# Seven block products for the values of two attention groups in a hybrid decoder block on Trainium2

## The chip, the cores and the metric

The kernel runs on one core of a Trainium2 chip. The metric is the device time of one execution in microseconds (us); the time of the kernel before is the median of 3 runs. The engines are named as in the profile: PE multiplies matrices, DVE works on vectors, ACT computes functions and copies, POOL is the general engine, SP issues most of the transfers. PEld is PE's loading of weights, which runs beside its matmuls.

## The reference, cut to what matters

One decoder layer: a SwiGLU half, a token-mixing part, a second SwiGLU half, a final norm. The change is in the token mixing. `u` is 512 tokens by 1024 features, all in float32.

```python
def token_mixing(u, cos, sin, w_in, w_pool, pool_scale, w_pool_branch, w_attn_branch, w_out):
    proj = u @ w_in
    p, q, k, v, gate_logits = jnp.split(proj, cuts, axis=-1)
    y_pool = multiscale_pool(p, w_pool, pool_scale)
    ...
    for gi, (window, dilation) in enumerate(ATTN_PATTERNS):   # (128, 1), (512, 4), (2048, 16)
        hs = slice(gi * HEADS_PER_GROUP, (gi + 1) * HEADS_PER_GROUP)
        o, lse = dilated_window_attention(q[:, :, hs], k[:, :, hs], v[:, :, hs], window // dilation, dilation)
    ...
    gates = jax.nn.sigmoid(gate_logits)
    g_pool, g_attn = jnp.split(gates, N_BRANCHES, axis=-1)
    merged = g_pool * (y_pool @ w_pool_branch) + g_attn * (y_attn @ w_attn_branch)
    return merged @ w_out
```

There are three groups of four heads of 64. The values of groups 2 and 3 are one product: the 512 tokens of `u` by 1024 by 512 columns of `w_in`. The gates are another product of the same `u`, by 2048 columns.

## The kernel before

**Precision.** Every float32 operand is held as a high part and a low part (`UH` and `UL` for `u`, `whi` and `wlo` for weights). A product of two operands is three matmuls: high by high, high by low, low by high.

**Weights.** SP loads them in chunks of 128x1024 into three buffers `raw`. For each chunk ACT writes the high part (line 377) and DVE subtracts it to get the low part (line 389); both go into the ring `whi`/`wlo`. `look(n)` prepares n chunks ahead of the one that PE takes.

**Seven products.** Where the code says `blocks`, a matrix product is split into 2x2 blocks and done by seven block products instead of eight (a Strassen scheme). Four chunks r11, r12, r22, r21 are loaded and seven are used: r11; x0 = r12 + r11; x1 = r22 + x0; r21; r12 + r22; r22; x1 + r21. The first two sums are made on DVE (`make`, line 312). The last two are made by transfers that add to their target and that POOL issues (`add`, line 320): the first when x1 has been made, the second when r21 has been split. The other operand needs four such sums too; `mix_sums` makes them from the parts of `u`: `whole` adds high and low part, `x0`, `x2`, `x1`, `x3` combine the blocks, `hi` and `lo` split the results for PE, and `last` writes the fourth over a block of `UH` and `UL`. A product is 24 matmuls of 128x256; the result of each goes from its bank in PSUM to a copy, since the next product but one accumulates in the same bank.

**Order of the token mixing.** Python code emits it and each engine keeps that order. After the queries and keys of group 1 and its values come eight tiles of 24 matmuls of 128x512 (`mm_tile`): the queries and keys of groups 2 and 3. Two such tiles follow for the pooling; after each, POOL computes `pool_diff` (lines 1573 to 1594). Then come the values of groups 2 and 3: four chunks of 128 tokens, 24 matmuls of 128x512 each (lines 1765 to 1767), with their weights as four chunks held at once; DVE copies each from its bank to `v23` (line 1768). Then come the gates: `gate_duo`, seven products that give two columns of tiles of each gate, four times with branch products between.

**Attention in steps.** The attention of groups 2 and 3 is done in four classes of 128 strided tokens. A class passes through scores on PE (`at_scores`), mask and maximum on DVE and exponentials on ACT (`at_exp`), transposes on PE (`at_turn`, copied by ACT) and values on PE (`at_values`). `hooks` puts the values of one class, the transposes of the next and the scores of a third into one gap between matmuls. Before, class 0 has its scores in the second pooling tile, its transposes in the first chunk of the values and its values in the second; class 3 ends after the first product of the first gate.

**Background.** A row of conditioning products (`bg`, one DVE instruction over 128x1024 and one load each) fills gaps on DVE. A `settle` is a dummy matmul of 128x240 ahead of some products.

Of the kernel before, what the change touches and what calls it, by code (L numbers as in the profile page):

```python
# [18 lines left out]
KT = 8  # L19
# [87 lines left out]
def lay_mix(w_in, w_pb, w_ab, w_out):  # L107
# [16 lines left out]
    for i in range(4):  # L124
        ch.append(v[2 * i:2 * i + 2, :, 256:].transpose(1, 0, 2).reshape(P, -1))
# [40 lines left out]
class Kernel:  # L166
# [6 lines left out]
    def plan(self):  # L173
# [86 lines left out]
        plain(mx[:20])  # L260
# [7 lines left out]
        self.beside = range(base + 4, base + 6)  # L268
# [12 lines left out]
        self.units.update({base + i: T for i in range(16, 20)})  # L281
# [458 lines left out]
    def product(self, bank, u, start, extra=0, other=None):  # L740
# [4 lines left out]
        for p in range(2):  # L745
            o = bank[:, p * HT:(p + 1) * HT]
            for k in range(4):
                (hi, lo), (uh, ul) = w[4 * p + k], u[k]
                M(o, hi, uh, start=start and p == 0 and k == 0, stop=False, skip_group_check=True)  # L749
                M(o, hi, ul, start=False, stop=False, skip_group_check=True)  # L750
                M(o, lo, uh, start=False, stop=k == 3, skip_group_check=True)  # L751
# [557 lines left out]
    def mix_sums(self, xs, x3, slots):  # L1309
# [3 lines left out]
        H, L = {}, {}  # L1313
        four = lambda y: y.rearrange("p (k t) -> p k t", k=4)
        w = xs[:, :2 * D].rearrange("p (k h t) -> p k h t", k=4, h=2)
        x = [four(xs[:, 2 * D:]), w[:, :, 0], w[:, :, 1], four(x3)]

        def copies():
            nc.sync.dma_start(xs[:, :2 * D], self.UHv[:, :2 * D].bitcast(F32))

        def adds():
            nc.gpsimd.dma_start(xs[:, :2 * D], self.ULv[:, :2 * D].bitcast(F32), accum_op=OP.add)

        def whole(i):
            ts = slice(0, HT) if i else slice(HT, T)
            v.tensor_tensor(x[i], *(y.rearrange("p (k t) -> p k t", k=KT)[:, 4:, ts] for y in (self.UHv, self.ULv)), op=OP.add)

        def hi(i):
            H[i] = slots[i][0]()
            nc.scalar.activation(four(H[i]), x[i], AF.Copy)  # L1330

        def lo(i):
            L[i] = slots[i][1]()
            v.tensor_tensor(four(L[i]), x[i], four(H[i]), op=OP.subtract)
            self.S[i] = [H[i], L[i]]
# [4 lines left out]
        def last():  # L1340
            nc.scalar.activation(self.S[3][0], x[3], AF.Copy)
            sub(self.S[3][1], x[3], self.S[3][0])

        self.S = [None] * 3 + [[y.rearrange("p (k t) -> p k t", k=KT)[:, :4, HT:] for y in (self.UHv, self.ULv)]]
        return dict(copies=copies, adds=adds, x0=lambda: sub(x[0], x[0], x[2]), x2=lambda: sub(x[2], x[1], x[2]),
                    x1=lambda: minus(x[1], x[0], x[1]), whole=whole, x3=lambda: minus(x[3], x[3], x[1]), hi=hi, lo=lo, last=last)
# [226 lines left out]
    def pool_diff(self, t, bank):  # L1573
# [4 lines left out]
        if t:  # L1578
            p = self.v23.rearrange("p c f -> p (c f)")[:, 2 * T:2 * T + 528]
# [20 lines left out]
    def pool_map(self, high, low):  # L1600
# [3 lines left out]
        banks = (self.bO, self.bS[0])  # L1604
# [10 lines left out]
    def mix(self):  # L1615
# [8 lines left out]
        xs = mp.tile([P, 3 * D], F32, name="xs")  # L1624
        x = [xs[:, i * D:(i + 1) * D] for i in range(3)]
        two = lambda n: [t[:, i * T:(i + 1) * T] for t in [mp.tile([P, D], F32R, name=n)] for i in range(2)]
# [3 lines left out]
        with tc.tile_pool(name="rt", bufs=1) as self.rt, tc.tile_pool(name="aw", bufs=2) as self.aw:  # L1630
# [22 lines left out]
            self.ada_free, self.ada_stop, self.ada_depth = list(x), 59, 2  # L1653
# [57 lines left out]
            for g in (1, 2):  # L1711
                for dst in (self.qt[g], self.kt[g]):
                    for hp in range(2):
                        more = [(2, self.bg)] if dst is self.qt[1] and hp else []
                        b = self.mm_tile(hooks(todo.pop(0), rest + more + [(7, self.bg)]))
                        rt = [self.scratch(2 * i + hp)[:, :T] for i in range(2)]
                        self.rope_a(b, dst, hp, *rt)

                        rest = [(6, lambda dst=dst, hp=hp, w=rt[1]: self.rope_b(dst, hp, w))]


            g23 = [[(1, c, hp) for hp in range(2)] for c in range(4)]
            b = self.mm_tile(hooks([], rest + [(3, self.bg)]))
            self.pool_diff(0, b)
            assert self.ada_next == 59 and not self.adat, self.ada_next
            self.ada_free, self.ada_stop, self.ada_depth = [self.cs], 60, 1
            self.bg_fetch()
            v4 = []

            def half(i):  # L1730
                if not v4:
                    v4.append(ma.tile([P, 2 * D], F32R, name="v23"))
                return v4[0][:, i * D:(i + 1) * D]

            u = self.mix_sums(xs, self.qt[2], [[wide(ma, "k2"), wide(mp, "uc")], [wide(ma, "k0"), wide(ma, "v1")],
                                                 [lambda: half(0), lambda: half(1)]])
# [4 lines left out]
            assert self.ada_next == 60 and not self.adat, self.ada_next  # L1741
            self.held = self.pos
            w = [x for _ in range(4) for x in self.take()]
# [6 lines left out]
            def free():  # L1750
                self.held += 1
# [445 lines left out]
```

## Time and profile before

| what | before |
|---|---|
| median of 3 runs | 970.66 us (970.06 to 971.09) |
| the profiled execution | 969.99 us |
| its span, first to last instruction | 968.2 us |
| PE busy | 958.5 us (99%) |
| DVE busy | 840.3 us (87%) |
| ACT busy | 539.3 us (56%) |
| POOL busy | 89.8 us (9%) |

The profile comes from one execution. A row of the timeline has the start, the duration, the engine, the line, the operation, output<-inputs with their shape, the number of merged instructions and, in brackets, the idle time before it with what ended it. A row of a group has the busy time in all and the mean of one in ns. Matmuls overlap in PE's pipeline, so what one costs is read from the distance between starts. In the trace, `v` is both `v1` and `v23`, and the last digits of names are left out.

### The profile page before, as it was taken

Reading aid. Unit: us, or ns where it says so; the run is one execution under the profiler, and the core shown is the slowest. Engines: PE = TensorE matmul, PEld = TensorE weight load, DVE = VectorE, ACT = ScalarE, POOL = GpSimd, SP = SyncE. Lnnn points to the kernel's source line nnn. Section 1 sums busy time; section 2 is a strip of 40 time slices with the busy share of each in tenths; the row PEclk is TensorE's granted clock in tenths of the full one; section 3 lists DMA queues with packets and bytes.
Section 4 is the critical chain, followed back from the end, with each engine's and each line's share of the span. In section 5 each row is a group of like instructions: output and inputs, shape, how many; then the busy total and the mean of one; then the engine's idle time right before and its main releaser. Section 6 shows DMA issues by size and latency. Waiting matters only on the chain.

```text
span 968.2 us, 18169 instructions
## 1 busy us (share of the span) xinstructions
PE 958.5 (99%) x7296; PEld 899.9 (93%) x7296; DVE 840.3 (87%) x1237; ACT 539.3 (56%) x813; POOL 89.8 (9%) x106
## 2 busy tenths in 40 slices
PE   9999999999999999999999999999999999999997
PEld 7888999999999899778889998998999999999997
DVE  7989999899998778787897877989799888989886
ACT  5443666665755553444565453365666747566655
POOL 0000110101010003005510000000101000110002
PEclk9999999999999999999999999999999999999999
DMA  9857785776768648766457445723757666665632
GB/s 353 283 178 257 197 239 156 202 212 153 219 176 246 171 148 238 239 206 188 90 141 199 124 126 207 243 73 104 194 141 198 170 157 167 172 171 143 169 83 88
DMA packets 54087, 174.71 MB, mean 180 GB/s; under 512 B 7793, under 2 KB 10481, under 8 KB 53746
## 3 DMA queue, kind: packets, MB, share of 16 engines
q1 hardware_dynamic: 44416, 141.29, 44.2%
q0 software_dynamic: 9008, 31.72, 18.1%
q8 instruction: 57, 0.93, 0.4%
q10 hardware_dynamic: 578, 0.53, 0.2%
q14 instruction: 28, 0.23, 0.1%
HBM read 135.36 MB, written 2.24 MB: 142 GB/s over the span
## 4 chain that ended last, share of the span: by engine, by line
PE 84%; DVE 7%; DMA 4%; issue 2%; ACT 1%; POOL 0%; SPq 0%; POOLq 0%; DVEq 0%; ACTq 0%
PE bank L750 13%; PE bank L749 12%; PE bank L751 12%; PE bank L421 7%; PE bank L422 7%; PE bank L423 7%; PE bank L1109 4%; PE bank L1108 4%; PE bank L1110 4%; DVE wlo L389 2%; PE bank L2119 2%; PE bank L2121 1%; PE bank L2123 1%; DMA v<-wada 1%; DMA cs<-wada 1%
## 5 line engine op out<-in xcount | busy, mean ns | idle before, releaser
L389 DVE TENSOR_TENSOR wlo<-raw,whi 128x1024 fp32r<-128x1024 f32 (+3 forms) x150 | 166.4, 1118 | 37.7 <-ACT whi L377 37.5
L749 PE MATMUL bank<-UH,whi 128*128 128x256 f32 x672 | 185.7, 276 | 0.0
L750 PE MATMUL bank<-UL,whi 128*128 128x256 f32 x672 | 185.6, 276 | 0.0
L751 PE MATMUL bank<-UH,wlo 128*128 128x256 f32 x672 | 185.6, 276 | 0.0
L389 DVE TENSOR_TENSOR wlo<-X,whi 128x1024 fp32r<-128x1024 f32 (+3 forms) x133 | 142.2, 1082 | 17.8 <-ACT whi L377 17.6
L377 ACT ACTIVATE whi<-raw 128x1024 fp32r<-128x1024 f32 (+3 forms) x150 | 142.6, 964 | 22.1 <-DMA raw<-wf1o 8.4
L377 ACT ACTIVATE whi<-X 128x1024 fp32r<-128x1024 f32 (+3 forms) x133 | 123.0, 946 | 51.0 <-DVE X L312 46.1
L750 PEld LDWEIGHTS bank<-UL,whi 128*128 128x128 f32 x672 | 126.3, 188 | 0.0
L749 PEld LDWEIGHTS bank<-UH,whi 128*128 128x128 f32 x672 | 126.1, 188 | 0.2
L751 PEld LDWEIGHTS bank<-UH,wlo 128*128 128x128 f32 x672 | 126.2, 188 | 0.0
L751 PE MATMUL bank<-SH,wlo 128*128 128x256 f32 x408 | 112.7, 276 | 0.2 <-DVE wlo L389 0.2
L749 PE MATMUL bank<-SH,whi 128*128 128x256 f32 x408 | 112.6, 276 | 0.0
L750 PE MATMUL bank<-SL,whi 128*128 128x256 f32 x408 | 112.6, 276 | 0.0
L421 PE MATMUL bank<-UH,whi 128*128 128x512 f32 (+1 forms) x272 | 93.0, 342 | 0.0
L422 PE MATMUL bank<-UL,whi 128*128 128x512 f32 (+1 forms) x272 | 92.0, 338 | 0.0
L423 PE MATMUL bank<-UH,wlo 128*128 128x512 f32 (+1 forms) x272 | 91.8, 337 | 0.0
L751 PEld LDWEIGHTS bank<-SH,wlo 128*128 128x128 f32 x408 | 76.6, 188 | 0.4 <-DVE wlo L389 0.4
L749 PEld LDWEIGHTS bank<-SH,whi 128*128 128x128 f32 x408 | 76.6, 188 | 0.0
L750 PEld LDWEIGHTS bank<-SL,whi 128*128 128x128 f32 x408 | 76.6, 188 | 0.0
L1108 PE MATMUL bank<-HI,whi 128*128 128x256 f32 x224 | 61.8, 276 | 0.0
L1109 PE MATMUL bank<-HK,whi 128*128 128x256 f32 x224 | 61.8, 276 | 0.0
L1110 PE MATMUL bank<-HI,wlo 128*128 128x256 f32 x224 | 61.8, 276 | 0.0
(406 smaller groups left out, 2410.9 us busy)
## 6 DMA issues: line engine op xcount, KB each, us to landing
raw<-wmix SPq DMA_DIRECT2D x44, 512.0 KB, 4.3
raw<-wf1i SPq DMA_DIRECT2D x32, 512.0 KB, 5.9
raw<-wf2i SPq DMA_DIRECT2D x30, 512.0 KB, 4.3
ada<-wada SPq DMA_DIRECT2D x23, 512.0 KB, 5.2
X<-raw POOLq DMA_DIRECT2D x23, 512.0 KB, 6.0
xs<-wada SPq DMA_DIRECT2D x17, 512.0 KB, 5.3
X<-wf2i SPq DMA_DIRECT2D x14, 512.0 KB, 4.5
X<-wf1i SPq DMA_DIRECT2D x11, 512.0 KB, 4.6
```

Of the source, the lines that this page charges most:

```text
L377: self.nc.scalar.activation(self.hi[:, y], r[:, x], AF.Copy)
L389: self.nc.vector.tensor_tensor(self.lo[:, y], r[:, x], self.hi[:, y], op=OP.subtract)
L421: M(ps, hi, uh, start=start, stop=False)
L422: M(ps, hi, ul, start=False, stop=False)
L423: M(ps, lo, uh, start=False, stop=stop)
L749: M(o, hi, uh, start=start and p == 0 and k == 0, stop=False, skip_group_check=True)
L750: M(o, hi, ul, start=False, stop=False, skip_group_check=True)
L751: M(o, lo, uh, start=False, stop=k == 3, skip_group_check=True)
L1108: M(o, hi, uh, start=start and m % 2 == 0 and k == 0, stop=False, skip_group_check=True)
L1109: M(o, hi, ul, start=False, stop=False, skip_group_check=True)
L1110: M(o, lo, uh, start=False, stop=k == 1, skip_group_check=True)
L2119: M(b, hi, self.UH[k], start=k == 0, stop=False)
```

## The change

The values of groups 2 and 3 become seven block products. Their four weight chunks are laid out as 2x2 blocks (four rows of 128 by 256 columns) and planned with `blocks`. A new function `value_duo` runs them: 168 matmuls of 128x256 instead of 96 of 128x512. The stationary operand is a block of `u` or of its sums, the moving one the weights.

- The sums of `u` are the ones that the first gate uses. They are needed earlier now and are made in the last two tiles of queries and keys and the two pooling tiles. All four blocks are added from high and low part by DVE (`whole`); the load of `UH` by SP and the adding transfer of `UL` by POOL go.
- The background rows there go from 14 to 11; rows 56 to 59 move into the first two gates.
- The results leave their banks by six copies on ACT and two subtractions on DVE, instead of four copies on DVE.
- The attention of the classes starts later: scores of class 0 in the middle of the third product, then a step in the middle of the fifth and the seventh, and of the first gate's second, fourth and sixth. The merge of the groups comes after the first gate.
- The dummy matmuls of the first gate go.

The core of the diff:

```diff
@@ lay_mix
-    for i in range(4):
-        ch.append(v[2 * i:2 * i + 2, :, 256:].transpose(1, 0, 2).reshape(P, -1))
+    for i, c in ((0, 256), (0, 512), (4, 512), (4, 256)):
+        ch.append(v[i:i + 4, :, c:c + 256].transpose(1, 0, 2).reshape(P, -1))
@@ plan
-        plain(mx[:20])
+        plain(mx[:16])
+        blocks(mx[16:20], True)
@@ mix
+            sums = {6: [(7, lambda: u["whole"](0))], 7: [(1, lambda: u["whole"](2)), (4, u["x0"]), (6, lambda: u["hi"](0)),
+                                                         (7, lambda: u["whole"](1))]}
...
+            b = self.mm_tile(hooks([], rest + [(1, u["x2"]), (3, u["x1"]), (5, lambda: u["lo"](0)), (7, lambda: u["whole"](3))]))
             self.pool_diff(0, b)
...
-            b = self.mm_tile(hooks(g23[0], [(3, u["copies"]), (4, u["adds"]), (7, self.bg)]))
+            b = self.mm_tile(hooks([], [(0, lambda: u["hi"](1)), (0, lambda: u["hi"](2)), (1, u["x3"]), (3, lambda: u["lo"](2)),
+                                      (5, lambda: u["lo"](1))]))
             self.pool_diff(1, b)
...
-            for c in range(4):
-                hk = hooks(g23[c + 1] if c < 3 else [], [(k, f) for n, k, f in beside if n == c])
-                b = self.nb()
-                for k in range(KT):
-                    for f in hk.get(k, ()):
-                        f()
-                    (hi, lo), uh, ul = w[k], *(x[k][:, c * P:c * P + P] for x in (self.UH, self.UL))
-                    M(b, uh, hi, start=k == 0, stop=False)
-                    M(b, uh, lo, start=False, stop=False)
-                    M(b, ul, hi, start=False, stop=k == KT - 1)
-                v.tensor_copy(self.v23[:, c, :], b)
...
+            step = lambda c=None: [lambda: [f() for f in hooks(g23[c] if c is not None else [])[5]]]
+            p5 = self.ev[:, 2 * T:3 * T]
+            self.value_duo(p5, {1: u["last"]}, {2: step(0), 4: step(1), 6: step(2)})
...
             used = self.gate_duo(self.qt[1], self.kt[1], p5, lambda n=1: None,
+                                 {2: lambda: (self.at_swap(), rows()), 3: clear, 4: self.bg, 5: self.bg, 6: third}, {},
+                                 {1: step(3), 3: step(), 5: step()})
@@ value_duo
+        for i, (bank, u, start) in enumerate(((A, lambda: blk(0, 0), True), (B, lambda: self.S[0], True),
+                                              (A, lambda: self.S[1], False), (C, lambda: blk(4, 0), False),
+                                              (A, lambda: self.S[2], False), (B, lambda: blk(0, HT), False),
+                                              (A, lambda: blk(4, HT), False))):
+            self.look(3 if i in (0, 2) else 4)
+            w, x = self.take(), u()
+            for c in range(2):
+                o = bank[:, c * 256:c * 256 + 256]
+                for f in within.get(i, ()) if c else ():
+                    f()
+                for k in range(4):
+                    (hi, lo), (uh, ul) = w[k], (y[:, c * P:c * P + P] for y in x[k])
+                    M(o, uh, hi, start=start and c == k == 0, stop=False, skip_group_check=True)
+                    M(o, uh, lo, start=False, stop=False, skip_group_check=True)
+                    M(o, ul, hi, start=False, stop=k == 3, skip_group_check=True)
+            if i == 0:
+                copy(C, A)
+            elif i == 1:
+                copy(p5, B)
+            elif i == 2:
+                copy(self.v23[:, T1, F2], r(A), -1.0)
+            elif i == 3:
+                copy(self.v23[:, T1, F1], r(C))
+            elif i == 4:
+                copy(self.v23[:, T2, F2], r(A), -1.0)
+            elif i == 5:
+                v.tensor_tensor(self.v23[:, T1, F2], self.v23[:, T1, F2], r(B), op=OP.subtract)
+                v.tensor_tensor(self.v23[:, T2, F2], self.v23[:, T2, F2], r(p5), op=OP.subtract)
+            elif i == 6:
+                copy(self.v23[:, T2, F1], r(A))
```

How POOL's queue is ordered at the two pooling differences, before. Row 38 ends the first difference, row 39 is the adding transfer of `UL` for the sums of `u`, row 40 begins the second difference:

```order
37 L1596 TENSOR_TENSOR ev<-rt_4437,cst 64x16
38 L1597 TENSOR_TENSOR ev<-ev,tr 64x512
39 L1322 DMA xs<-UL 128x2048
40 L1581 MEMSET v_3520 128x16
41 L1588 TENSOR_TENSOR rt_4501<-v_3520 128x527
```

The same place now. Row 39 is the transfer that adds r22 to r12 of the values' weights, for the fifth product:

```order
37 L1593 TENSOR_TENSOR ev<-rt_4441,cst 64x16
38 L1594 TENSOR_TENSOR ev<-ev,tr 64x512
39 L321 DMA raw_65<-raw_63 128x1024
40 L1578 MEMSET rt_4496 128x16
41 L1585 TENSOR_TENSOR rt_4494<-rt_4496 128x527
```

And the end of the second difference now. Row 51 adds r21 to x1 (held in `cs`) for the seventh product of the values; rows 52 and 53 belong to the first gate:

```order
48 L1592 TENSOR_SCALAR ev<-rt_4495 64x496
49 L1593 TENSOR_TENSOR ev<-rt_4495,cst 64x16
50 L1594 TENSOR_TENSOR ev<-ev,rt_4496 64x512
51 L321 DMA cs<-raw_64 128x1024
52 L321 DMA raw_63<-raw_64 128x1024
```

What moved: both transfers that the values' own weights wait for stand behind a pooling difference in POOL's queue; before, the values' weights needed no transfer of POOL.

DVE before, around the second chunk of the values: the copy of the first chunk, the low part of a gate's weights, the copy of a class's attention, and then the mask of the next class (`ISA` rows):

```order
527 L1474 TENSOR_SCALAR negmax<-st 128x2
528 L1768 COPY v_3520<-bank_96 128x512
529 L389 TENSOR_TENSOR wlo<-raw_65,whi 128x1024
530 L1513 COPY q_3513<-bank_97 128x2x128
531 L1472 ISA prob,st<-bank_93,masks 128x256
```

DVE now, from the low part of the seventh product's weights (row 533) on: the first gate's sums and low parts, then the mask of class 1:

```order
532 L1471 TENSOR_SCALAR negmax<-st 128x2
533 L390 TENSOR_TENSOR wlo<-cs,whi 128x1024
534 L313 TENSOR_TENSOR AR<-raw_63,raw_65 128x1024
535 L390 TENSOR_TENSOR wlo<-raw_65,whi 128x1024
536 L313 TENSOR_TENSOR cs<-raw_64,AR 128x1024
537 L390 TENSOR_TENSOR wlo<-AR,whi 128x768
538 L390 TENSOR_TENSOR wlo<-AR,whi 128x256
539 L1469 ISA prob,st<-bank_93,masks 128x256
```

The rows behind that mask, up to the two subtractions that complete `v23` (bank 91 holds the second and sixth product):

```order
548 L1471 TENSOR_SCALAR negmax<-st 128x2
549 L390 TENSOR_TENSOR wlo<-cs,whi 128x1024
550 L1847 TENSOR_TENSOR v_3522<-v_3522,bank_91 128x2x256
551 L1848 TENSOR_TENSOR v_3522<-v_3522,ev 128x2x256
552 L390 TENSOR_TENSOR wlo<-raw_65,whi 128x1024
```

What moved: before, only one low part stood between a copy of values and the next mask; now six instructions of the weights stand between row 533 and the mask of class 1, and one more ahead of the subtractions.

ACT now, from the high part of the seventh product's weights (row 319) to the copy of the fifth product out of its bank (row 327):

```order
319 L378 ACTIVATE whi<-cs 128x1024
320 L378 ACTIVATE whi<-raw_65 128x1024
321 L1815 ACTIVATE v_3522<-bank_95 128x2x256
322 L378 ACTIVATE whi<-AR 128x768
323 L378 ACTIVATE whi<-AR 128x256
324 L1489 ACTIVATE probT<-bank_90 128x512
325 L1489 ACTIVATE probT<-bank_92 128x512
326 L1474 ACTIVATE prob,st<-prob,negmax 128x256 x4
327 L1815 ACTIVATE v_3522<-bank_96 128x2x256
```

ACT before, at the second chunk of the values, where no copy out of a bank of the values is in its queue:

```order
312 L377 ACTIVATE whi<-raw_65 128x1024
313 L1492 ACTIVATE probT<-bank_90 128x512
314 L1492 ACTIVATE probT<-bank_92 128x512
315 L1477 ACTIVATE prob,st<-prob,negmax 128x256 x4
316 L377 ACTIVATE whi<-AR 128x1024
```

What moved: the copy that frees bank 96 for the seventh product stands behind the four exponentials of class 1.

More of the change, by code (lines that the diff above doesn't have):

```diff
@@ L738, in later, with product @@
         self.put.append((self.now + n, f))
-    def product(self, bank, u, start, extra=0, other=None):
+    def product(self, bank, u, start, extra=0, other=None, within=()):
         M = self.nc.tensor.matmul
@@ L1829, in gate_duo @@
             self.look(3 if i in (0, 2) else 4)
-            self.product(bank, u(), start, i in settles, settles.get(i))
+            self.product(bank, u(), start, i in settles, settles.get(i), within.get(i, ()))
             if i == 0:
```

155 lines of the change are left out of this document (66 added, 89 removed).

## The prediction

> **What bounds the kernel now.** I read the head of the page first, then PE's waits, then PE's timeline in the stage of the change, and last the timelines of POOL, DVE and ACT there.
>
> ```profile
> span 968.2 us, 18169 instructions
> PE 958.5 (99%) x7296; PEld 899.9 (93%) x7296; DVE 840.3 (87%) x1237; ACT 539.3 (56%) x813; POOL 89.8 (9%) x106
> PE bank L2020 <- DVE ones L2025: 1.1, 1, 1.1
> ```
>
> PE is the bound: it is busy for 99%, and its longest wait anywhere is 1.1 us, at the start. So the change is worth what it takes off PE's list, less whatever wait it puts there. What a matmul costs is the distance of starts:
>
> ```profile
> 450.95 0.39 PE L1765 MATMUL bank<-whi,UH 128*128 128x512 f32 x1
> 452.99 0.39 PE L1765 MATMUL bank<-whi,UH 128*128 128x512 f32 x1
> ...
> 483.98 0.28 PE L749 MATMUL bank<-UH,whi 128*128 128x256 f32 x1
> 486.69 0.28 PE L751 MATMUL bank<-UH,wlo 128*128 128x256 f32 x1
> ...
> 493.60 0.28 PE L749 MATMUL bank<-UH,whi 128*128 128x256 f32 x1
> 496.32 0.28 PE L749 MATMUL bank<-v,whi 128*128 128x256 f32 x1
> ```
>
> The first pair are nine matmuls of 512 columns apart: 2.04 / 9 = 0.227 us each. The last pair are 24 of 256 columns, one product: 2.72 us, 0.113 each. The middle pair are 23 apart: 0.118 each, a slower pace that some stretches have.
>
> **The change part by part.** *Matmuls.* 96 x 0.227 = 21.8 us go and 168 x 0.113 = 19.0 us come: 2.7 us less on PE. At the slower pace the fourteen products of values and first gate would cost 14 x 24 x 0.0045 = 1.5 us more; I take the faster pace and keep 1.5 for the range.
>
> *Dummy matmuls and gaps.*
>
> ```profile
> 487.92 0.38 PE L427 MATMUL bank<-UH,whi 128*128 128x240 f32 x1
> 488.14 0.28 PE L749 MATMUL bank<-k,whi 128*128 128x256 f32 x1
> 463.12 1.09 PE L1489 MATMUL bank<-cst,prob 128*128 128x128 f32 x8
> 464.15 1.16 PE L1456 MATMUL bank<-k,q 64*128 64x128 f32 x16
> ```
>
> A dummy ends 0.22 us later, of which about half is the restart after the gap that any matmul there would pay; two of them go, -0.2 us. The attention's matmuls are the same and keep their six gaps, but the pooling map and the transposed factors now have one each: +0.2 us. These cancel, and PE's list is 2.7 us shorter.
>
> *When PE wants the weights.* Transposes cost 1.0 us (463.12 to 464.15) and scores 1.1, with 0.2 for the gap. The second pooling tile loses its scores (1.3), so the first product starts at 450.95 - 1.3 = 449.65. Six products (16.3 us), the scores in the third (1.3) and transposes with scores in the fifth (2.3) put the start of the seventh at 469.6 and its gap for class 0's values at 471.0.
>
> *POOL.* The fifth product's weights wait for an adding transfer behind the first pooling difference, the seventh's for one behind the second.
>
> ```profile
> 444.44 1.07 ACT L1582 ACTIVATE tr<-bank 128x512 f32<-128x512 f32 x1 [5.05 <-issue]
> 445.66 1.06 POOL L1588 TENSOR_TENSOR rt<-tr 128x527 f32<-128x527 f32 x1 [8.16 <-ACT tr L1582]
> 446.80 1.93 POOL L1588 TENSOR_TENSOR rt<-rt 64x525 f32<-64x525 f32 x1
> 448.80 1.46 POOL L1595 TENSOR_SCALAR ev<-rt 64x496 f32<-64x496 f32 x1
> 450.24 0.21 POOL L1596 TENSOR_TENSOR ev<-rt,cst 64x16 f32<-64x16 f32 x1
> 451.91 2.40 POOL L1595 TENSOR_SCALAR ev<-rt 64x496 f32<-64x496 f32 x1
> 454.67 1.27 POOL L1597 TENSOR_TENSOR ev<-ev,tr 64x512 f32<-64x512 f32 x1
> 455.89 0.96 POOL L1322 DMA_DIRECT2D xs<-UL  x1
> 461.86 2.33 POOL L1595 TENSOR_SCALAR ev<-rt 64x496 f32<-64x496 f32 x1
> 467.33 2.87 POOL L1596 TENSOR_TENSOR ev<-rt,cst 64x16 f32<-64x16 f32 x1
> 470.28 2.23 POOL L1597 TENSOR_TENSOR ev<-ev,v 64x512 f32<-64x512 f32 x1
> 472.45 0.92 POOL L320 DMA_DIRECT2D raw<-raw  x1
> ...
> 451.78 1.21 DVE L448 SCALAR_TENSOR_TENSOR cs<-cs,cond 128x1024 f32<-128x1024 f32 x1
> 454.84 2.19 DVE L389 TENSOR_TENSOR wlo<-raw,whi 128x1024 fp32r<-128x1024 f32 x1 [1.84 <-ACT whi L377]
> ```
>
> POOL starts when the first pooling tile's copy is done, and nothing ahead of that changes. It needs until 472.45 for both differences with one issue between. In that time it and DVE hold each other up: POOL's 2.40 beside DVE's 1.21 is 1.46 when alone, and DVE's low part at 454.84 takes 2.19 beside POOL's 1.27, and one takes 1.12 on average (page row below). POOL's five stretched rows (1.93, 2.40, 2.33, 2.87, 2.23) against the same forms alone (1.06, 1.46, 1.46, 0.21, 1.27) hold 6.3 us of such waiting. With none POOL would end at 466.1. Now DVE has ten sums and low parts in a row between the rope's addition and the fifth product's low part, but then stands still while it waits for the first adding transfer. With one DVE instruction ahead of six more of POOL's 18 it is 472.45 + 6 x 1.12 = 479.2. I take the end of before, 472.45, between 466.1 and 479.2.
>
> *From there to PE.* Prices of the steps:
>
> ```profile
> raw<-raw POOLq DMA_DIRECT2D x2, 512.0 KB, 6.1
> L389 DVE TENSOR_TENSOR wlo<-raw,whi 128x1024 fp32r<-128x1024 f32 (+3 forms) x150 | 166.4, 1118 | 37.7 <-ACT whi L377 37.5
> L377 ACT ACTIVATE whi<-raw 128x1024 fp32r<-128x1024 f32 (+3 forms) x150 | 142.6, 964 | 22.1 <-DMA raw<-wf1o 8.4
> 473.52 1.21 DVE L1326 TENSOR_TENSOR xs<-UH,UL 128x1024 f32<-128x1024 f32 x1
> 448.88 0.42 DVE L1472 CUSTOM_DVE_ANT_0 prob<-bank,masks 128x256 f32<-128x256 f32 x1 [1.08 <-PE bank L1456]
> 450.57 1.29 DVE L1474 TENSOR_SCALAR negmax<-st 128x2 f32<-128x2 f32 x1
> 452.41 0.49 ACT L1477 ACTIVATE prob<-prob,negmax 128x256 f32<-128x256 f32 x1
> 487.01 0.58 ACT L1814 ACTIVATE bank<-bank 128x512 f32<-128x512 f32 x1 [2.10 <-PE bank L751]
> 484.51 0.68 DVE L1768 COPY v<-bank 128x512 f32<-128x512 f32 x1
> ```
>
> Transfer 6.1, high part 0.96, low part 1.12: 480.6. That alone would let the seventh product start 11 us late. But it must also wait for ACT's copy of the fifth product out of its bank, which stands behind the exponentials of class 1, which need DVE's mask, which stands behind the low part just named. On DVE follow two sums and two low parts (2 x 1.21 + 2 x 1.12 = 4.7): 485.3. The mask of a class takes from 448.88 to 450.57 and 0.2 for its last instruction: 487.2. The last two exponentials 1.0, the copy 0.6: the seventh product starts at 488.8, 19.2 us late. In its middle, at 490.2, class 0's values need the first subtraction on `v23`: high part 0.96, low part 1.12, subtraction 0.68 after 488.8 make 491.5, another 1.4 us (the copy of the same size stands for the subtraction). The first transfer's chain (class 0's mask and the copy of the third product) delays the fifth product in the same way by less than the slack that remains before the seventh. So +20.6 us of wait.
>
> *The rest.* The sums of `u` cost DVE two `whole` more (2.4 us) and remove two transfers; the four background rows moved cost 4 x 1.21 us of DVE in the gates, where PE's products of 2.72 us hide them (at most 4.8 us if DVE were late there too). The first gate's weights are ready while PE waits, so nothing is late after `v23`. All of this I cost at nothing.
>
> Sum: 20.6 - 2.7 = +17.9 us on the profiled execution's 969.99: 987.9. That execution is 0.67 us under the median of the runs, so 988.6 in the terms of that median. With POOL ending at 466.1 it is 6.3 us less (982.3); at 479.2, 6.7 us more (995.3).
>
> **The rivals.** *The clock drops in the waits.* PE would stand idle for several us at a time, twice or three times, which it never does now.
>
> ```profile
> 1.06 2.50 PE L2020 MATMUL bank<-ones 128*128 128x128 f32 x10 [1.06 <-DVE ones L2025]
> 3.70 2.33 PE L2045 MATMUL bank<-X,ones 128*128 128x512 f32 x4
> 5.87 1.39 PE L2054 MATMUL bank<-ones,AR 128*128 128x128 f32 x11
> ```
>
> At the start PE runs at half pace: ten matmuls take 2.50 us where eleven take 1.39 a little later; it lasts from 1.06 to 5.87. After a wait that does the same, 4.8 us of work at half pace cost 2.4 us; the loss after the fifth product's wait falls into the seventh's, so +2.4, 991.0, or 4.8 with both. The Trainium skill, TensorE: Matmul & The Clock Gate, Part 1, says that an idle window of about 3.4 us throttles PE and a busy one releases it; no wait in this trace is long enough to show it. Chance 0.25.
>
> *The transfers come in time.* Were POOL's two differences and transfers done before DVE needs their sums, DVE's own list would decide. From the end of the rope's addition at 444.69 (row below) it has 17 sums and low parts of about 1.15 and one mask of 1.9 up to the mask of class 1: 466.1. Mask, exponentials and copy (1.9 + 1.0 + 0.6) end at 469.6, in time, and the last three steps as above at 472.4, against 471.0.
>
> ```profile
> 444.00 0.69 DVE L1423 TENSOR_TENSOR k<-k,rt 128x512 f32<-128x512 f32 x1
> ```
>
> That gives 1.4 - 2.7 = -1.3, 969.4, the same within what can be told. Against it: POOL cannot end before 466.1, and with 8.2 us from there to the low part the seventh product is late by itself. Chance 0.05.
>
> *The gain stands.* If in addition the mask of class 1 and the subtraction are out of the way (DVE ahead of that list by 1.4 us), PE's shorter list is all that counts: 968.0. It decides once the seventh product's low part is ready by 460.0 (471.0 less 2.8, 0.6, 1.0, 1.9 and 4.7). For it speaks only that PE is busy for 99% now; POOL's rows speak against. Chance 0.05.
>
> **How the numbers follow.** The forecast, with POOL's end anywhere between its bounds, has 0.65; the clock 0.25; the two cases without waits 0.05 each. A run under or over another by 0.2% (1.9 us) is about what a measurement of this kernel can tell from no change. Slower: 0.65 + 0.25 = 0.90; same 0.05; faster 0.05. The range takes in the lower bound of POOL's end, less the 6.6 us of sums and mask, should these not lie in series behind the low part (982.3 - 6.6 = 975.7, so 976), and the upper bound with most of one clock loss (995.3 + 1.7 = 997). Predicted time: 988.6.
>
> **What would show it.** PE would have idle time of 15 to 25 us between 445 and 500, put down to ACT or DVE at the third, fifth and seventh products of the values; POOL's two adding transfers would start after 454 and after 466; DVE's low part from `cs` for the seventh product would start after 474; starts of the 168 matmuls would be 0.113 us apart elsewhere. The prediction is wrong if the seventh product starts within 3 us of the sixth's end, or if POOL's transfers stand ahead of the differences in time. The clock rival shows as distances of twice 0.113 us after a wait.

## The result and the profile after

The changed kernel takes 997.9 us (median of 6 runs, 996.14 to 999.62) against 970.14 us of the kernel before in the same runs: a ratio of 1.0288, 95% interval 1.0272 to 1.0303. It is 2.9% slower. The forecast was 988.6 with a range up to 997.0: the sign and two thirds of the size came out, and the result lies just above the range.

The head of the page after. The row `PEclk` is the granted clock of PE, in tenths of full speed, in 40 slices of 24.9 us:

```profile
span 996.9 us, 18353 instructions
PE 968.9 (97%) x7366; PEld 912.9 (92%) x7366; DVE 850.0 (85%) x1255; ACT 548.5 (55%) x837; POOL 91.6 (9%) x107
PEclk9999999999999999998798999999999999999999
```

PE is busy for 10 us more, though its list is shorter, and the clock, which stood at 9 everywhere before, is at 8, 7 and 8 in slices 19, 20 and 22, from 449 us on. More than half of the loss is waits (PE's idle time went from 9.7 to 28.0 us), and much of the rest is matmuls at half pace. PE's waits, with total, count and longest:

```profile
PE bank L1833 <- ACT v L1815: 9.0, 2, 4.9
PE bank L1544 <- DVE f L1538: 3.6, 1, 3.6
PE bank L1835 <- DVE x L1331: 2.5, 1, 2.5
PE bank L1833 <- ACT bank L1815: 1.4, 1, 1.4
```

Lines 1833 to 1835 are the matmuls of the values: 12.9 us of waits in place of none. The 3.6 us at line 1544 (the transposes of the merge's factors) are outside the values, and no term of the forecast had them. Where the waits stand on PE's timeline:

```profile
452.29 0.28 PE L1833 MATMUL bank<-whi,UH 128*128 128x256 f32 x1
455.11 0.28 PE L1833 MATMUL bank<-whi,uc 128*128 128x256 f32 x1
...
462.52 0.58 PE L1835 MATMUL bank<-whi,x 128*128 128x256 f32 x1 [2.46 <-DVE x L1331]
462.90 0.41 PE L1833 MATMUL bank<-whi,k 128*128 128x256 f32 x1
463.11 0.41 PE L1834 MATMUL bank<-wlo,k 128*128 128x256 f32 x1
...
475.73 0.58 PE L1833 MATMUL bank<-whi,v 128*128 128x256 f32 x1 [4.09 <-ACT v L1815]
...
491.31 0.39 PE L1833 MATMUL bank<-whi,UH 128*128 128x256 f32 x1 [4.94 <-ACT v L1815]
...
533.84 1.88 PE L1544 MATMUL bank<-cst,f 128*8 128x128 f32 x8 [3.61 <-DVE f L1538]
```

The third, fifth and seventh product wait. After the first of these waits the starts are 0.21 us apart (462.90 to 463.11), nearly twice 0.113. The seventh product starts 491.31 - 452.29 = 39.02 us after the first one; without waits it would be 19.95 (469.6 - 449.65, from the forecast).

POOL's two adding transfers, and behind the second one the chain on ACT and DVE:

```profile
461.31 0.96 POOL L321 DMA_DIRECT2D raw<-raw  x1
476.16 0.92 POOL L321 DMA_DIRECT2D cs<-raw  x1
...
480.79 1.06 ACT L378 ACTIVATE whi<-cs 128x1024 fp32r<-128x1024 f32 x1 [5.11 <-DMA cs<-raw]
481.88 1.23 DVE L390 TENSOR_TENSOR wlo<-cs,whi 128x1024 fp32r<-128x1024 f32 x1 [7.90 <-ACT whi L378]
487.63 0.42 DVE L1469 CUSTOM_DVE_ANT_0 prob<-bank,masks 128x256 f32<-128x256 f32 x1
490.68 0.57 ACT L1815 ACTIVATE v<-bank 128x512 f32<-128x512 f32 x1
```

This is the forecast chain step by step: transfer, high part, low part, two sums and two low parts of the first gate's weights (481.88 to 487.63 with the low part; in the order of DVE above these are the five rows 534 to 538, since one low part takes two), mask, exponentials, copy, product.

The place that it missed, at the first branch product. SP issues the load of a background row and then that of the weights; ACT's high part waits for these; DVE does the low part, the pooling factors (L1610), then the merge (L1538). The first line is from SP's waits between 495 and 540 us: twice, 7.8 us at the longest, SP stands at a row's load until DVE is through with the row before, and the weights' load stands behind it.

```profile
SPq L441 <- DVE q L449: 11.9, 2, 7.8
...
522.81 0.33 SPq L441 DMA_DIRECT2D q<-wada  x1
523.19 0.45 SPq L296 DMA_DIRECT2D raw<-wmix  x1
...
527.90 1.06 ACT L378 ACTIVATE whi<-raw 128x1024 fp32r<-128x1024 f32 x1 [6.37 <-DMA raw<-wmix]
529.00 1.22 DVE L390 TENSOR_TENSOR wlo<-raw,whi 128x1024 fp32r<-128x1024 f32 x1 [0.53 <-ACT whi L378]
530.74 1.40 DVE L1610 SCALAR_TENSOR_TENSOR x<-bank,vecs,k 128x512 fp32r<-128x512 f32 x2
533.61 0.17 DVE L1538 TENSOR_TENSOR f<-e,d 128x16 f32<-128x16 f32 x1
```

**A ruler for what follows.** Ahead of the values PE's instructions are the same in the changed kernel and in every experiment, yet the first product starts anywhere from 446.9 to 452.3 us in their profiled executions. So each edit is read from lengths inside the trace: from the first product's start to the seventh's (A), from the first product's start to the first branch product of line 422 behind the second gate (B), and from there to the norm's first matmul of line 520 (C). Each length is of one execution; the medians are of all. The kernel before took 968.28 to 970.14 us beside the runs, and each ratio is to the one beside it. Of the kernel before, the first product is put at 449.65, as in the forecast, and its lines are 421 and 519.

| run | A | B | C | median us | ratio to before, 95% |
|---|---|---|---|---|---|
| before | (19.95 without waits) | 78.9 | 102.7 | 970.14 | 1 |
| after | 39.0 | 103.5 | 104.0 | 997.90 | 1.0272 to 1.0303 |
| 1 POOL later | 31.5 | 96.3 | 104.3 | 987.81 | 1.0168 to 1.0198 |
| 2 mask first | 34.4 | 99.8 | 105.3 | 991.99 | 1.0213 to 1.0244 |
| 3 merge early | 39.0 | 103.4 | 104.2 | 993.96 | 1.0223 to 1.0259 |
| 4 dummy matmuls | 39.8 | 101.8 | 104.0 | 993.28 | 1.0225 to 1.0260 |
| 5 steps moved | 31.7 | 95.8 | 104.4 | 988.30 | 1.0175 to 1.0208 |
| 6 = 1 with 5 | 24.4 | 90.5 | 104.5 | 981.62 | 1.0111 to 1.0147 |
| 7 = 6, merge, bank | 23.8 | 90.0 | 104.1 | 981.99 | 1.0113 to 1.0157 |
| 8 no differences | 24.1 | 89.1 | 104.8 | 979.86 | 1.0099 to 1.0140 |
| 9 rows later | 39.0 | 98.6 | 110.3 | 997.19 | 1.0281 to 1.0314 |
| 10 all, rows later | 22.7 | 84.6 | 111.0 | 983.84 | 1.0137 to 1.0168 |
| 11 = 7, no rows | 23.0 | 87.6 | 102.8 | 976.90 | 1.0065 to 1.0094 |
| 12 = 11, no differences | 20.5 | 79.4 | 102.4 | 971.39 | 1.0014 to 1.0036 |

### The profile page after: what moved, and what is told of

Read it like the earlier page. It is cut to its first block, busy times and chain, and to the rows that moved or that the text cites. A ratio compares the mean times of both kernels' runs of the same rounds, so it can differ in the third digit from the quotient of the medians.

```text
span 996.9 us, 18353 instructions
## 1 busy us (share of the span) xinstructions
PE 968.9 (97%) x7366; PEld 912.9 (92%) x7366; DVE 850.0 (85%) x1255; ACT 548.5 (55%) x837; POOL 91.6 (9%) x107
## 4 chain that ended last, share of the span: by engine, by line
PE 78%; DVE 8%; issue 4%; DMA 4%; POOL 3%; ACT 2%; SPq 0%; POOLq 0%; ACTq 0%; DVEq 0%
PE bank L752 11%; PE bank L754 11%; PE bank L753 11%; PE bank L422 8%; PE bank L423 8%; PE bank L424 8%; PE bank L1113 4%; PE bank L1111 4%; PE bank L1112 4%; DVE wlo L390 2%; PE bank L2122 1%; PE bank L2124 1%; PE bank L2126 1%; DMA cs<-wada 1%; DMA raw<-wmix 1%
```

## The experiments

My theory at this point was that the values lose 19 us to POOL's queue and the chain behind it, and that 7 more go at the merge. The rivals were that DVE's own order alone sets the seventh product's start, that the clock losses of the three waits add up, and that the merge is only late because all ahead of it is.

**1. POOL's arithmetic behind the transfers.** `pool_diff` keeps ACT's copy; POOL's part runs after the first product.

```diff
-            self.value_duo(p5, {1: u["last"]}, {2: step(0), 4: step(1), 6: step(2)})
+            late = lambda: [self.pool_late(t) for t in range(2)]
+            self.value_duo(p5, {0: late, 1: u["last"]}, {2: step(0), 4: step(1), 6: step(2)})
```

> POOL's arithmetic of both pooling differences is emitted after the first product of the values, so both adding transfers of the values' weights stand ahead of it in POOL's queue; nothing else changes. Theory of the queue (both transfers come late because they stand behind the differences): the first transfer starts near 455 instead of 461.3, the second near 460 instead of 476.2, the seventh product starts about 14 us earlier (near 477 instead of 491.3), and 10 to 15 us of the 28 go: 983 to 988 us. Rival (DVE's own order, six instructions of the weights ahead of the mask, sets the seventh product's start whatever POOL does): within 3 us of 998. Second rival (DVE and POOL hold each other up just as much at the later place): 990 to 994.

Measured: 987.81 us, inside the expected range, but not as expected: A is 7.5 us shorter, not 14, and of the 10 us that the median fell, 3 lie outside B and C. The transfers came even earlier than expected, and yet the fifth product waits for 3.6 us and the seventh for 5.1. POOL and DVE of this run:

```profile
446.67 0.92 POOL L321 DMA_DIRECT2D raw<-raw  x1 [62.74 <-DVE AR L313]
450.51 0.88 POOL L321 DMA_DIRECT2D cs<-raw  x1 [2.92 <-DVE wlo L390]
...
465.36 2.05 DVE L390 TENSOR_TENSOR wlo<-cs,whi 128x1024 fp32r<-128x1024 f32 x1 [2.69 <-ACT whi L378]
467.33 2.07 DVE L313 TENSOR_TENSOR AR<-raw,raw 128x1024 f32<-128x1024 f32 x1
469.33 2.33 DVE L390 TENSOR_TENSOR wlo<-raw,whi 128x1024 fp32r<-128x1024 f32 x1
471.57 1.61 DVE L313 TENSOR_TENSOR cs<-raw,AR 128x1024 f32<-128x1024 f32 x1
```

The same DVE instructions that took 1.22 to 1.23 in the changed kernel (481.88) take 1.6 to 2.3 beside POOL's arithmetic, which now runs here. The queue is real, and only a part.

**2. The mask of class 1 ahead of the first gate's sums.**

```diff
-            self.look(3 if i in (0, 2) else 4)
+            self.look((3, 4, 3, 2, 2, 2, 2)[i])
```

> From the fourth product of the values on, weights are prepared two products ahead instead of four: on DVE the mask of class 1 then follows directly on the low part of the seventh product's weights, and the two sums and two low parts of the first gate's weights come behind it; POOL's queue is as in the changed kernel. Theory of the chain (those four stand in series between the second transfer and the seventh product): the seventh product starts 4.5 us earlier, near 486.8, its wait falls under 1 us, and with the slow clock behind that wait 5 to 7 us go: 991 to 993 us. Rival (the transfer alone decides): 998. If the first gate's weights are late in their turn, the loss shows there and the time is 995 to 998.

Measured: 991.99 us, A 4.7 us shorter, the wait at the seventh product gone but for 0.3 us: as the theory of the chain has it. The wait at the merge grew from 3.6 to 4.7 us: 1.4 of the 5.2 us that were won at the end of the values were lost again there. Class 0's values now wait 0.8 us for the subtraction.

**3. The merge two products earlier.**

```diff
-                self.at_merge()
...
-                                 {2: lambda: (self.at_swap(), rows()), 3: clear, 4: self.bg, 5: self.bg, 6: third}, {},
+                                 {2: lambda: (self.at_swap(), rows()), 3: clear, 4: lambda: (self.at_merge(), self.bg()), 5: self.bg, 6: third}, {},
```

The first sigmoid moves from the fourth product's end behind that.

> The merge of the groups' factors goes from behind the first gate's seventh product to behind its fifth, ahead of the gate's first sigmoid, which comes at the same place; the values and their waits stay as in the changed kernel. Theory (the forecast missed this wait of 3.6 us for the factors at the transposes and the half clock behind it, 7 us in all): 990 to 992 us, the two loads of ACT's tables at the merge gone, and PE's row at the transposes without a wait. Rival (the merge only waits because everything ahead is late, and the wait moves elsewhere): within 2 us of 998.

The median fell to 993.96 us, but A, B and C are those of the changed kernel within 0.2 us, so the difference lies ahead of the values (the first product starts at 448.36 in place of 452.29) and is not the edit's. The wait at line 1544 has another releaser:

```profile
PE bank L1544 <- DVE x L1610: 2.9, 1, 2.9
```

The transposes go into a bank from which the pooling factors (line 1610) are still read. The merge itself is done at 519.6 here, 9 us before that reading starts. So the theory of a merge in the wrong place falls: what is late there is what DVE does behind one low part.

**4. Dummy matmuls in the waits.**

```diff
             w, x = self.take(), u()
+            for _ in range({2: 36, 4: 56, 6: 70}.get(i, 0)):
+                M(self.bO[:, :256], self.UH[0][:, :P], self.UH[4][:, :256], start=True, stop=True, skip_group_check=True)
```

> Dummy matmuls of 256 columns into a bank that nobody reads stand ahead of the third (36), fifth (56) and seventh (70) product of the values, so that PE has work through most of its waits; all else is as in the changed kernel. Theory (the seventh product's start is set by POOL and DVE, so the slow clock after the two earlier waits is swallowed by the next wait, and only what runs slow after the last wait counts): 2 to 3 us go, 995 to 996 us. Rival (the losses of all three waits add up): 7 to 8 us go, 990 to 991. If the clock does not depend on PE standing idle: 998, or more where the dummies outlast the wait.

The mean clock rose from 0.985 to 0.997. A did not get shorter (39.8 against 39.0), though the sixth product starts 28.6 us after the first in place of 31.1. The dummies outlast the last wait a little, but the copy that frees the bank ends only 39.5 us after the first product (39.0 in the changed kernel), so the chain holds the seventh product as before. B fell by 1.7 us, none of it in the values: class 0's values now wait for the subtraction instead (0.6 us, below), and the gain is at the merge. The median is 993.28 us, under the expected 995 to 996; of the 4.6 us more than half is neither in B nor in C. The losses do not add up; the chain swallows them.

```profile
PE bank L1544 <- DVE f L1538: 2.9, 1, 2.9
PE bank L1504 <- DVE v L1849: 0.6, 1, 0.6
```

**5. The attention steps of classes 0 and 1 at the second and fourth product,** with weights prepared two products ahead as in run 2.

```diff
-            self.value_duo(p5, {1: u["last"]}, {2: step(0), 4: step(1), 6: step(2)})
+            self.value_duo(p5, {1: u["last"]}, {1: step(0), 3: step(1), 6: step(2)})
```

> The attention steps of classes 0 and 1 go from the third and fifth product of the values into the second and fourth, whose results are not the ones that the next product waits for; weights are prepared two products ahead from the third on, so the mask of class 1 stands ahead of the low part of the seventh product's weights on DVE. POOL's queue is as in the changed kernel. Theory (behind the second transfer, which still starts near 476, only a high part and a low part are left before the seventh product, and after them two instructions ahead of the subtractions): the fifth product's wait goes, the seventh starts 8 us earlier, 988 to 991 us. If the in-order chains on ACT and DVE are all that holds PE, the transfers included in nothing: 978 to 982.

Measured: 988.30 us, A 7.4 us shorter. The fifth and the seventh product no longer wait, but class 0's transposes in the fourth do, since its mask stands on DVE behind the low part that waits for the first transfer:

```profile
PE bank L1486 <- ACT prob L1474: 4.7, 1, 4.7
```

**6. Runs 1 and 5 together.**

> Both earlier edits at once: POOL's arithmetic of the differences after the first product of the values, and the attention steps moved as in the run beside it. Theory: POOL's queue and the order behind the transfers hold the values together, so all three waits of the values fall under 1 us each, the merge's wait of 4 to 5 us with the half clock behind it stays, and so does a wait of 1.3 us in the second gate: 970 - 2.7 + 7 + 2 + 1 to 3 for what DVE loses to POOL, 976 to 980 us. If DVE and POOL holding each other up is the larger part, POOL's new place beside the low parts costs as much as the queue did and the time is 983 to 987.

Measured: 981.62 us, between the two ranges. A is 24.4, so 4.4 of the 19.1 us are left: 1.8 of wait at class 0's transposes, and half pace behind it. The wait at the merge is 5.3 us now, longer than without the gains ahead of it.

**7. Run 6 with the merge early** and the transposes in the bank of the attention's values.

```diff
-            spread = [self.bS[1], self.bO] + self.bT
+            spread = [self.bO, self.bS[1]] + self.bT
```

> The run beside it, and the merge ahead of the first gate's first sigmoid, with the transposed factors in the bank of the attention's values instead of one that the pooling factors are still read from (in the run that only moved the merge, the transposes waited 2.9 us for that reading). Theory: the wait at the transposes goes too, PE's list is 2.7 us shorter than in the kernel before, and 1 to 4 us of small waits are left: 968 to 972 us, the same as before within what can be told. If moving the merge only moves the wait on to the next product: 974 to 977.

Measured: 981.99 us, as run 6. The expectation of 968 to 972 was wrong: the wait moved on to the next instruction, a dummy matmul in another bank of the pooling factors.

```profile
PE bank L428 <- DVE x L1614: 3.9, 1, 3.9
```

**8. The pooling differences' arithmetic left out.** In `pool_diff` all of it becomes `g.memset(d, 0.0)`.

> The changed kernel with the arithmetic of both pooling differences left out (POOL only fills the two results with zeros), so the pooling branch of the output is not computed. Against the run that only put this arithmetic behind the transfers, it also takes away what DVE and POOL cost each other. Theory (the queue was worth 10 us; the rest of the waits at the fifth and seventh product, 3.9 and 5.4 us, is half DVE's low parts stretched beside POOL and half the order on DVE and ACT): 980 to 984 us. Rival (with the transfers early, only the order on DVE and ACT holds the products): 987 to 988 as in that run.

Measured: 979.86 us, just under the expected range. A is 24.1 against 31.5 of run 1, which has the transfers early too: POOL's arithmetic beside the values costs 7.4 us. The rows of run 1 are back at their short times:

```profile
464.28 1.23 DVE L390 TENSOR_TENSOR wlo<-cs,whi 128x1024 fp32r<-128x1024 f32 x1 [2.69 <-ACT whi L378]
465.42 1.22 DVE L313 TENSOR_TENSOR AR<-raw,raw 128x1024 f32<-128x1024 f32 x1
466.56 1.22 DVE L390 TENSOR_TENSOR wlo<-raw,whi 128x1024 fp32r<-128x1024 f32 x1
```

So DVE and POOL do hold each other up. The Trainium skill, SBUF — State Buffer, in "SBUF: two separate sides", says that a POOL instruction that reads SBUF and a DVE instruction with two SBUF inputs contend for one pair of ports, and that the loser blocks for the whole instruction; the rows of run 1 (2.05 to 2.33 in place of 1.22) and these 7.4 us agree.

**9. The four background rows done behind the gates,** with the last twelve.

```diff
-                                 {2: lambda: (self.at_swap(), rows()), 3: clear, 4: self.bg, 5: self.bg, 6: third}, {},
+                                 {2: self.at_swap, 3: clear, 6: third}, {},
...
-                for _ in range((2, 2, 3, 2, 1)[m]):
+                for _ in range((3, 3, 4, 3, 1)[m]):
```

> The changed kernel with the four background rows 56 to 59 taken out of the first two gates and done with the last twelve, behind the gates; all else stays. Theory (the rows cost DVE little, but their loads stand in SP's queue ahead of the gate's weights and share one buffer, so each waits for DVE to finish the row before; the weights of the first branch product land late at 527.9 and with them the pooling factors and the merge): the wait of 3.6 us at the transposes falls under 1 us and 4 to 7 us go, 991 to 994 us. Rival (the rows are as cheap as the forecast put them and the merge waits for its own place on DVE): 997 to 999.

The time is 997.19 us, as the rival had it, and yet the rows are the cause: B is 4.9 us shorter, the wait at the transposes is 1.0, and C is 6.3 us longer, since PE now waits at the end of the mixing.

```profile
PE bank L424 <- DVE wlo L390: 4.6, 2, 3.5
PE bank L1544 <- DVE f L1538: 1.0, 1, 1.0
```

**10. All edits,** with two products of preparation throughout and the subtractions directly behind the seventh product's low part.

> All edits at once: POOL's arithmetic behind the transfers, steps moved, weights prepared two products ahead throughout the values with the subtractions directly behind the seventh product's low part, the merge early with its own bank, and the background rows behind the gates. Theory: of the 12 us that the run without the last two of these is over the kernel before, 7 go with the rows and 3 to 4 with the waits at class 0's transposes and values: 970 to 973 us, not faster than before. If the wait at the first branch product has another cause: 976 to 980.

Measured: 983.84 us, not the expected 970 to 973. B is 5.4 us shorter than in run 7 and C 6.9 longer: the rows are paid at the end again, which the expectation had overlooked.

**11. Run 7 without the rows.**

> The run with the steps moved, POOL later and the merge early in its own bank, now with the background rows 56 to 59 left out altogether (their four modulation values are set to zero, so that part of the output is not computed), and the subtractions directly behind the seventh product's low part. Theory (the rows' loads and DVE time hold the weights of the first branch product, wherever the merge stands): the wait of 3.9 us there, the half clock behind it (3.3) and the wait of 1.5 us in the second gate go, and nothing is paid at the end of the mixing: 973 to 976 us. If the wait there comes from the late start of the attention alone: 980 to 982.

Measured: 976.90 us, 0.9 over the expected range. The profile is of the slowest of the six executions (981.57 us). C is back at 102.8, and the waits at the merge and in the second gate are gone. One wait is new and comes from this edit: the copy of the seventh product stands behind the exponentials of class 2, for which the first gate waits.

```profile
PE bank L752 <- ACT v L1819: 4.0, 1, 4.0
```

**12. Run 11 without the differences too.**

> The run beside it with the arithmetic of the pooling differences left out as well (POOL fills the results with zeros; pooling branch and four modulation values are not computed), so that neither POOL's queue nor its sharing with DVE is left. Theory (PE's list is 2.7 us shorter, and with DVE and POOL out of the way only small waits remain): 968 to 971 us. If PE's list is not shorter than before (the slower pace of 0.118 us, more gaps): 971 to 974. If waits of 5 us and more remain in the values, something else than DVE, POOL and the order of steps holds them.

Measured: 971.39 us, still 0.25% over the kernel before: just over the expected range, and inside the one for a list of PE that is no shorter. The profile is of the fastest of the twelve executions (969.24 us), and speaks for a shorter one. A is 20.5, 0.5 over what PE needs. B is 79.4; without that same wait (2.0, and 0.2 for the restart) 77.2, which is 1.7 us under the kernel before, 2.2 without the 0.5 in A.

```profile
PE bank L752 <- ACT v L1805: 2.0, 1, 2.0
```

## Why the prediction was right or wrong

The profiled spans differ by 28.7 us: 2.6 lie ahead of the first product (452.29 against 449.65), 24.6 in B, 1.3 in C. The 24.6 are 19.1 (A) + 1.3 (class 0's values) + 6.4 (merge) - 2.2 (PE's list, from run 12). The forecast had 19.2 + 1.4 - 2.7.

- **PE's list, -2.7.** Right in kind; run 12 shows 2.2. Some products go at the slower pace: from 452.29 to 455.11 are 24 matmuls, 0.1175 each, the bound that I had kept apart. That is all that the change could win with DVE, POOL and the rows out of the way, and the median of run 12 does not show it.
- **The seventh product, 39.15 us after the first.** Measured 39.02. The single steps were less exact: POOL's second transfer started 29.1 us after the first pooling tile's copy (447.09 in the trace) where I had 28.0, and its data were there 4.6 us later where I had 6.1. Runs 1, 2, 5 and 8 show that queue, shared time of DVE and POOL, and order behind the transfers each hold the product: early transfers alone win 7.5 us, no POOL arithmetic 7.4 more, two products of preparation ahead of the mask 4.7. They overlap, so they don't add up.
- **The fifth product's chain inside the slack.** Right in effect, by run 4: what is lost before the seventh product's start costs nothing. In place it was wrong: the third product waits too, 1.4 us for ACT's copy of the first and 2.5 us for the low part of a sum of `u`; the list of signs named it, but the sum had both at nothing.
- **Class 0's values, +1.4.** The first subtraction ends 2.7 us after the seventh product's start, as forecast. But PE does not wait for it: half pace from 491.31 on (1.3 us more for twelve matmuls) brings PE to them only when the subtraction is done. That the two are of one size is luck.
- **"Nothing is late after `v23`", with the background rows at nothing and at most 4.8 us.** This is the step that failed. PE waits 3.6 us for the merge and then runs at half the clock until 539.34, 5.5 us that cost 2.8: 6.4 us. A further wait of 1.35 us in the second gate makes the 1.3 of C; it is gone in runs 9 to 12, where these rows are not in the gates. The rows that moved are four (45 to 59 stood ahead of the values before, 15 in all and not 14). I had counted the rows' DVE time, which PE's products would hide, and not their loads: they stand in SP's queue ahead of the gate's weights, and one buffer holds them all, so a load cannot start before DVE is through with the row before. Run 9 shows that the rows make the wait, and runs 9 and 10 that they cost as much at the end of the mixing. That it is the load in SP's queue, more than DVE's 1.2 us, is read from the traces: SP stands 7.8 us at the row's load, and issues the weights' load 70.9 us after the first product; in run 9 it issues the same load 63.8 us after it. From issue to ACT's high part are 4.7 us in the one and 5.3 in the other, so that load was issued late and was not slower. An edit of the loads alone was not tried.
- **The clock rival, 0.25.** Its mechanism is there (mean clock 0.985), and its count of one wait, the last one, was right for the values; half pace behind the merge's wait came on top. Its size was not: it reckoned with 4.8 us at half pace behind a wait, and the stretches are 3.4 or 6.8 us long (below).
- **The 2.6 us ahead of the change** arise at one place. Counted by matmuls, the two traces are 0.2 us apart until 299.4 us and 2.6 from 331.7 us on; between them PE of after waits for 1.39 and 0.29 us and runs at half clock for 3.4 (the rows are in the last section). PE's instructions there are the same in both. Of the other profiled executions, only that of run 11 shows this, and its first product, at 452.10, is the only other one later than 450.4. What makes ACT late there in some executions stays open, and so does how often it does in those without a profile.

## What to carry to other kernels

A product that PE does in fewer columns is worth only what its operands leave: here about 2 us were to be won, and 25 were lost, since the chains of DVE, POOL and ACT that the new operands need were longer than PE's work beside them. When a step moves, follow each of its instructions through each queue that it passes, the loads through SP's as well as the arithmetic through DVE's, and ask which buffer the load waits for. A fix that removes one wait in a stretch with a full engine shows the next one, so judge it by the length of the stretch and of the one behind it, not by the wait.

## What the runs showed of the hardware

Waits much shorter than I had reckoned with put PE to half pace. In the changed kernel a wait of 1.39 us ahead of line 752, in the first half of the layer, was followed by one of 0.29 and then by matmuls 0.213 us apart for 3.3 us:

```profile
305.79 0.39 PE L752 MATMUL bank<-SH,whi 128*128 128x256 f32 x1 [1.39 <-ACT ev L759]
306.59 0.39 PE L754 MATMUL bank<-SH,wlo 128*128 128x256 f32 x1 [0.29 <-DVE wlo L390]
...
307.54 0.42 PE L754 MATMUL bank<-SH,wlo 128*128 128x256 f32 x1
310.31 0.41 PE L752 MATMUL bank<-SH,whi 128*128 128x256 f32 x1
```

In run 6 a wait of 1.5 us at line 1504 was followed by matmuls at the full pace. The granted clock says more. It changes in steps of 3.41 us: behind waits it is at 0.5 for one step or two, in the changed kernel for 3.41 us from 307.23 and 491.55 and for 6.83 us from 460.83, 474.49 and 532.51. Where the steps lie differs from one execution to the next. A row of the next view has a stretch, its length, the busy time of PE, PEld, DVE, ACT and POOL, and the granted clock:

```profile
303.82:307.23 3.41, 1.73 (x13) 1.33 (x12) 3.41 (x6) 3.03 (x4) 0.00 (x0) 1.00 0.62 190
307.23:310.65 3.42, 3.42 (x18) 3.42 (x18) 3.42 (x5) 0.93 (x2) 0.00 (x0) 0.50 0.99 352
```

The two short waits add up to half of the step ahead of the change: PE is busy for 1.73 of 3.41 us. Over all 14 profiles, behind each of the 28 steps at full clock in which PE was idle for 56% or more came half clock, and behind none of the 3873 in which it was idle for 43% or less; of the 13 between, 5 led to half clock. Full clock came back only behind a step with at most 5% idle time (33 of 33). Idle time is by the rows of the profile, where the ends of matmuls are modelled. The Trainium skill, TensorE: Matmul & The Clock Gate, Part 1, speaks of an idle window of about 3.4 us that runs freely. The traces agree on its length and on its free place; but it need not be idle throughout, and it is not the length of one wait alone that decides.
